# Summing the partial rows of the adaLN modulation: transposes and a VectorE reduction in place of float32 matmuls with a selector

## The chip, the cores and the metric

The kernel is written in a tile language for one Trainium2 chip and uses one of its cores. Times are device microseconds of one execution. TensorE (PE in the profile) does the matrix work, VectorE (DVE) and ScalarE (ACT) the elementwise work, GpSimd (POOL) some small steps, and SyncE (SP) issues most of the transfers.

## The reference

One layer of a diffusion backbone runs on 128 context tokens and 512 latent tokens, D_MODEL = 1024, all in float32. What matters here is the modulation (adaLN): two conditioning vectors, one for the latent tokens and one for the context, are turned into six vectors of 1024 each.

```python
mod = (jax.nn.silu(cond) @ w_ada + b_ada)[:, None, :]
sh1, sc1, g1, sh2, sc2, g2 = jnp.split(mod, 6, axis=-1)
h = _rms(x, norm_mix) * (1 + sc1) + sh1
mix, k, v = _mixer(h, rope, ctx_k, ctx_v, w_in, ...)   # attention and a gated convolution
x = x + g1 * mix
h2 = _rms(x, norm_ffn) * (1 + sc2) + sh2
gate, up = jnp.split(h2 @ w_gate_up, 2, axis=-1)
x = x + g2 * ((jax.nn.silu(gate) * up) @ w_down)
```

`sh1, sc1` are needed before the input projection of every token, `sh2, sc2` only before the feed-forward part.

## The kernel before

Activations lie with features on the partitions when they enter a matmul: `hH[k]` and `hL[k]` are the rounded high part and the remainder of the modulated input for the 128 features of block k (k = 0 to 7), 640 tokens wide. Most products are done as three matmuls on high and low parts (`mm3`, lines 155 to 157).

**The partial sums.** `cond_mm` (line 388) multiplies the two SiLU'd conditioning vectors, padded to 32 columns (`cp`), with a block of `w_ada`. The eight blocks of the contraction go to four different groups of 32 output rows (`g = k % 4`), so the result in PSUM has 128 rows: row 32 g + c holds a partial sum of group g for conditioning vector c, with c = 0, 1 in use. The four groups have still to be added, and the result has to be turned so that features lie on the partitions. Both are done by one float32 matmul for each 128 features: the copied rows `res` are the stationary operand and `sel[:, 0:2]` the moving one, where `sel` has a one in row 32 g + c of column c.

**Where this occurs.** First in the opening stage: the string P1SEQ lists its steps in order, and in it `a` k is `ada1_mm` (the partial sums of feature block k, shift and scale together), `b` k is `ada1_res` (VectorE copies them to `res`, line 433), `m` k is `ada1_mod` (two selector matmuls at line 440, then `mod_evict`), `h` k is `h_do` (ScalarE and VectorE make hF, hH and hL of block k from the turned input `xT`), and `q` k t is `q_mm` (the query projection of block k for the 128 tokens t). In this stage the order on VectorE, ScalarE, GpSimd and SyncE is that of the program too, as written in the string. Second in the attention and convolution stage: the generator `ada_all` (line 777) does the same for the sections 3 and 4 of the modulation, two halves of 512 columns each, four selector matmuls for one half, spread among the steps `F` of the string SEQ; the last half falls into the start of the output projection. There the order on TensorE is that of the program, and the order on the other engines is set by a scheduler with priorities.

**mod_evict** (lines 404 to 416) reads the sums: one VectorE multiplication with the norm gain into `modt` (line 411), an addition into `modA` (line 412), and an addition of the bias into `modB` (line 415). `h_do` uses modA and modB as scale and bias (lines 473 to 479).

**Other steps that the prediction names.** Line 323 loads the blocks `af` of w_ada for the opening stage, four buffers in turn, from SyncE's queue. Line 536 makes the low part `wl` of a loaded weight on VectorE, line 152 the low part of other split tiles (hL among them), line 248 that of the output projection's weights. Line 247 makes their high part on ScalarE. Line 834 is the exponential of attention (`pr`), 840 its division, 851 the transposes of `pr`, 868 the product with the values; line 875 evicts it to `t`, 890 adds its two halves to `of`, line 891 squares that to `osq`, which `att_rms` (line 940) sums with a column of ones on TensorE. Line 1220 is an addition of the feed-forward part.

Of the kernel before, what the change touches and what calls it, by code (L numbers as in the profile page):

```python
# [9 lines left out]
F32 = mybir.dt.float32  # L10
F32R = mybir.dt.float32r
AF = mybir.ActivationFunctionType
ALU = mybir.AluOpType
AX = mybir.AxisListType

P = 128
# [15 lines left out]
CG = 32  # L32
# [59 lines left out]
def build(ctx, tc, x_prompt, x_sample, c, cache_k, cache_v, c_ctx, norm_mix, norm_ffn, w_ada, b_ada,  # L92
# [3 lines left out]
    act, dve, pool, pe, sp = nc.scalar, nc.vector, nc.gpsimd, nc.tensor, nc.sync  # L96
# [23 lines left out]
    def T(tag, shape, dt=F32, bufs=1):  # L120
        seq[0] += 1
        return pools[where.get(tag, "A")][1].tile(list(shape), dt, tag=tag, bufs=bufs, name=f"{tag}_{seq[0]}")

    def PB(shape=(P, 512), dt=F32, tag="t"):
        seq[0] += 1
        if kept.get(tag):
            w = kept[tag].pop()
            n = 1
            for y in shape[1:]:
                n *= y  # L130
            w = w[:, :n] if tag != "s" else w
            if tag != "s" and len(shape) > 2:
                names = "abc"[:len(shape) - 1]
                w = w.rearrange("p (" + " ".join(names) + ") -> p " + " ".join(names), **dict(zip(names, shape[1:])))
            return w
        return pools["psum"][1].tile(list(shape), dt, tag=tag, bufs=pbufs[tag], name=f"p{tag}_{seq[0]}")
# [10 lines left out]
    def early(n):  # L147
        return tc.high_priority(n)
# [106 lines left out]
    def W(key):  # L255
        p = place[key]
        while not in_pre[0] and stream_at[0] < len(order):
            nxt = order[stream_at[0]][0][0]
            ahead = AO if nxt == "o" else AOP if nxt in ("g", "u", "op") else AHEAD
            if stream_at[0] > p + ahead or order[stream_at[0]][2] > phase[0]:  # L260
                break
            load_next()
        assert order[p][5] is not None, key
        return order[p][5]
# [33 lines left out]
    for gi, grp in enumerate(GROUPS):  # L298
# [5 lines left out]
        for j in range(2):  # L304
            for i0 in range(0, len(grp), 2):
                n = len(grp[i0:i0 + 2])
# [22 lines left out]
    ident = T("ident", (P, P))  # L329
# [52 lines left out]
    sel = T("sel", (P, CG))  # L382
# [3 lines left out]
    def cond_mm(out, k, w):  # L386
        g = k % 4
        pe.matmul(out[CG * g:CG * (g + 1)], cp[:, k], w, start=(k < 4), stop=(k >= KD - 4), skip_group_check=True)  # L388
# [16 lines left out]
    def mod_evict(i, f0, n, ps_sc, ps_sh):  # L405

        no = (V_MIX, V_FFN)[i]
        bo = (0, 24)[i]
        if ps_sc is not None:
            tmp = T("modt", (P, n, 2), F32, 2)  # L410
            dve.tensor_tensor(tmp, ps_sc, vec[:, no + f0:no + f0 + n].unsqueeze(2).to_broadcast([P, n, 2]), ALU.mult)
            dve.tensor_tensor(modA[i][:, f0:f0 + n, :], tmp,
                              nb[:, i, f0:f0 + n].unsqueeze(2).to_broadcast([P, n, 2]), ALU.add)
        if ps_sh is not None:
            dve.tensor_tensor(modB[i][:, f0:f0 + n, :], ps_sh,
                              vec[:, bo + f0:bo + f0 + n].unsqueeze(2).to_broadcast([P, n, 2]), ALU.add)
# [14 lines left out]
    def ada1_res(k):  # L431
        res = T("res", (P, 256), F32, 2)
        dve.tensor_copy(res, ada1[k])
        ada1[k] = res

    def ada1_mod(k):
        res = ada1.pop(k)
        mp = PB((P, 2, 1, 2), tag="c" if k < 2 else "t")
        for i in range(2):
            pe.matmul(mp[:, i, 0], res[:, i * P:(i + 1) * P], sel[:, 0:2], start=True, stop=True)  # L440
        mod_evict(0, k, 1, mp[:, 0], mp[:, 1])

    xT = T("xT", (P, KD, TOK))

# [132 lines left out]
    def q_evict(t):  # L577
# [3 lines left out]
        else:  # L581
            act.activation(qraw[t], qacc[t], AF.Copy)

    steps = {"r": x_norm, "s": x_scale, "c": late_consts, "w": w_hi, "l": w_lo, "p": lambda i: rows2_load(), "x": xT_do,
             "v": lambda i: (vec_do, vec2_do)[i](), "m": ada1_mod, "a": ada1_mm, "b": ada1_res, "d": spin,
             "n": h_rest, "E": q_evict, "R": lambda i: rope_tables()}
    in_pre[0] = True
    for x in P1SEQ.split():
        k = int(x[1:] if x[0] == "d" else x[1:2] or 0)
# [164 lines left out]
    def ada_all():  # L754
        for sec, j in ADA:
            rp = PB(tag="c")
            for h in range(4):
                w = W(("ada", sec, j, h))
                for i in range(2):
                    cond_mm(rp, 2 * h + i, w[:, i])  # L760
                if h == 1:
                    yield
            res = T("rs5", (P, 512))
            with early(RSP) if RSP else ExitStack():
                act.activation(res, rp, AF.Copy)
            if sec == 2:
                sp.dma_start(res[2:3], b_ada[0:1, sec * D + j * 512:sec * D + (j + 1) * 512])
            yield
            if sec == 2:
                for cc in range(2):  # L770
                    ps = PB(tag="c")
                    pe.matmul(ps, selT[:, cc], res, start=True, stop=True)
                    act.activation(g1[cc][:, j * 512:(j + 1) * 512], ps, AF.Copy)
            else:
                ps = PB((P, 4, 2), tag="c")
                for f in range(4):
                    pe.matmul(ps[:, f], res[:, f * P:(f + 1) * P], sel[:, 0:2], start=True, stop=True)
                if sec == 4:
                    mod_evict(1, 4 * j, 4, ps, None)
                else:  # L780
                    mod_evict(1, 4 * j, 4, None, ps)

    ada_gen = ada_all()

    def ada_some(n):
# [176 lines left out]
    for x in SEQ.split():  # L962
        if "." in x:
            n, i = (int(y) for y in x[1:].split("."))
# [347 lines left out]


tile_hymba = with_exitstack(build)

_INS = ["x_prompt", "x_sample", "c", "cache_k", "cache_v", "c_ctx", "norm_mix", "norm_ffn", "w_ada", "b_ada",
# [44 lines left out]
```

## Time and profile before

| | |
|---|---|
| Time, median of 3 runs | 758.66 us |
| Runs | 757.63, 758.73, 758.66 us |
| Profiled execution: from first to last instruction | 755.2 us |
| Profiled execution's own time outside the trace | not given; the median of the runs lies 3.46 us above the span |
| TensorE busy | 737.5 us, 98% |
| VectorE busy | 551.7 us, 73% |
| ScalarE busy | 378.8 us, 50% |
| Mean granted TensorE clock | 0.999 |

Busy times of TensorE overlap: a matmul's recorded duration includes time in which the next has begun, so the distance between the starts of neighbouring instructions tells what one costs. A float32 matmul appears as two records (two weight loads and two matmuls), a transpose and a matmul of the rounded type as one.

### The profile page before, as it was taken

Reading aid. Unit: us, or ns where it says so; the run is one execution under the profiler, and the core shown is the slowest. Engines: PE = TensorE matmul, PEld = TensorE weight load, DVE = VectorE, ACT = ScalarE, POOL = GpSimd, SP = SyncE. Lnnn points to the kernel's source line nnn. Section 1 sums busy time; section 2 is a strip of 40 time slices with the busy share of each in tenths; the row PEclk is TensorE's granted clock in tenths of the full one; section 3 lists DMA queues with packets and bytes.
Section 4 is the critical chain, followed back from the end, with each engine's and each line's share of the span. In section 5 each row is a group of like instructions: output and inputs, shape, how many; then the busy total and the mean of one; then the engine's idle time right before and its main releaser. Section 6 shows DMA issues by size and latency. Waiting matters only on the chain.

```text
span 755.2 us, 11953 instructions
## 1 busy us (share of the span) xinstructions
PE 737.5 (98%) x4618; PEld 665.2 (88%) x4618; DVE 551.7 (73%) x997; ACT 378.8 (50%) x745; POOL 42.6 (6%) x75
## 2 busy tenths in 40 slices
PE   7999899999999999999999999999999999999997
PEld 5678888988998887899998799998889998899986
DVE  5558877666666798779979778884678866788653
ACT  5356777667656534765552235553125541255410
POOL 2403101011000110100000000000000000000000
PEclk9999999999999999999999999999999999999999
DMA  9985133532432464031235313133113232222312
GB/s 290 294 236 163 51 104 102 165 92 91 159 107 91 133 224 138 1 112 54 81 118 157 108 58 110 58 111 112 56 56 104 67 112 78 62 86 84 112 56 83
DMA packets 101389, 84.52 MB, mean 112 GB/s; under 512 B 3502, under 2 KB 81650, under 8 KB 101332
## 3 DMA queue, kind: packets, MB, share of 16 engines
q1 hardware_dynamic: 100980, 83.39, 35.9%
q8 instruction: 36, 0.59, 0.3%
q0 software_dynamic: 352, 0.37, 0.3%
q14 instruction: 21, 0.17, 0.1%
HBM read 79.68 MB, written 2.75 MB: 109 GB/s over the span
## 4 chain that ended last, share of the span: by engine, by line
PE 83%; DVE 7%; ACT 5%; DMA 2%; issue 1%; SPq 1%; POOL 0%; ACTq 0%
PE pf L155 17%; PE pf L157 17%; PE pf L156 17%; PE pc L710 3%; PE pc L712 3%; PE pc L711 3%; PE po L868 3%; PE ps L824 2%; PE ph L155 2%; PE ph L157 2%; PE ph L156 2%; PE pc L388 2%; PE pt L851 2%; DMA wf<-in_w_in_dram 1%; PE ps L155 1%
## 5 line engine op out<-in xcount | busy, mean ns | idle before, releaser
L151 ACT ACTIVATE wh<-wf 128x512 fp32r<-128x512 f32 (+1 forms) x68 | 55.5, 816 | 81.1 <-PE pf L157 59.3
L155 PE MATMUL pf<-wh,gT 128*128 128x512 f32 (+1 forms) x225 | 86.9, 386 | 0.0
L156 PE MATMUL pf<-wl,gT 128*128 128x512 f32 (+1 forms) x225 | 86.5, 385 | 0.0
L157 PE MATMUL pf<-wh,gT 128*128 128x512 f32 (+1 forms) x225 | 86.5, 384 | 0.0
L710 PE MATMUL pc<-hH,wh 128*128 128x320 f32 x192 | 61.1, 318 | 0.0
L712 PE MATMUL pc<-hH,wl 128*128 128x320 f32 x192 | 59.3, 309 | 0.0
L711 PE MATMUL pc<-hL,wh 128*128 128x320 f32 x192 | 59.3, 309 | 0.0
L152 DVE TENSOR_TENSOR wl<-wf,wh 128x1024 fp32r<-128x1024 f32 (+1 forms) x34 | 39.4, 1160 | 25.2 <-ACT wh L151 22.1
L155 PE MATMUL pf<-T,wh 128*128 128x320 f32 x160 | 49.6, 310 | 0.5 <-ACT u L1191 0.5
L156 PEld LDWEIGHTS pf<-wl,gT 128*128 128x128 f32 x225 | 42.3, 188 | 8.6 <-issue 0.2
L155 PEld LDWEIGHTS pf<-wh,gT 128*128 128x128 f32 x225 | 42.3, 188 | 8.6 <-issue 0.2
L157 PEld LDWEIGHTS pf<-wh,gT 128*128 128x128 f32 x225 | 42.3, 188 | 8.3
L156 PE MATMUL pf<-T,wh 128*128 128x320 f32 x160 | 49.4, 309 | 0.0
L155 PE MATMUL pf<-T,wl 128*128 128x320 f32 x160 | 49.4, 309 | 0.0
L156 PE MATMUL pf<-T,wl 128*128 128x320 f32 x160 | 49.4, 309 | 0.0
L157 PE MATMUL pf<-T,wl 128*128 128x320 f32 x160 | 49.4, 309 | 0.0
L157 PE MATMUL pf<-T,wh 128*128 128x320 f32 x160 | 49.4, 309 | 0.0
L155 PE MATMUL pf<-B,wl 128*128 128x320 f32 x152 | 47.1, 310 | 0.0
L157 PE MATMUL pf<-B,wl 128*128 128x320 f32 x152 | 47.0, 309 | 0.0
L156 PE MATMUL pf<-B,wl 128*128 128x320 f32 x152 | 47.0, 309 | 0.0
L155 PE MATMUL pf<-B,wh 128*128 128x320 f32 x136 | 42.2, 310 | 1.5 <-DVE cu L1220 1.5
L151 ACT ACTIVATE wl<-wf 128x512 fp32r<-128x512 f32 x34 | 21.2, 625 | 41.6 <-PE pf L156 34.8
(306 smaller groups left out, 2058.7 us busy)
## 6 DMA issues: line engine op xcount, KB each, us to landing
wf<-in_w_gate_up_dram SPq DMA_DIRECT2D x44, 512.0 KB, 4.0
aw<-in_w_ada_dram SPq DMA_DIRECT2D x24, 512.0 KB, 4.1
wf<-in_w_down_dram SPq DMA_DIRECT2D x20, 512.0 KB, 3.3
wf<-in_w_in_dram SPq DMA_DIRECT2D x18, 512.0 KB, 5.5
af<-in_w_ada_dram SPq DMA_DIRECT2D x32, 256.0 KB, 6.4
x<-in_x_sample_dram SPq DMA_DIRECT2D x8, 512.0 KB, 6.2
wf<-in_w_out_dram SPq DMA_DIRECT2D x8, 512.0 KB, 4.4
wf<-in_w_ada_dram SPq DMA_DIRECT2D x8, 512.0 KB, 3.7
```

The source lines that it names most:

```text
L151: act.activation(hi, src, AF.Copy)
L152: dve.tensor_tensor(lo, src, f32(hi), ALU.subtract)
L155: pe.matmul(out, lh, rh, start=start, stop=False, skip_group_check=more)
L156: pe.matmul(out, lh, rl, start=False, stop=False, skip_group_check=more)
L157: pe.matmul(out, ll, rh, start=False, stop=stop, skip_group_check=more)
L388: pe.matmul(out[CG * g:CG * (g + 1)], cp[:, k], w, start=(k < 4), stop=(k >= KD - 4), skip_group_check=True)
L710: pe.matmul(acc, wh[:, k], hH[k][:, c0:c0 + n], start=(k == 0), stop=False)
L711: pe.matmul(acc, wh[:, k], hL[k][:, c0:c0 + n], start=False, stop=False)
L712: pe.matmul(acc, wl[:, k], hH[k][:, c0:c0 + n], start=False, stop=(k == KD - 1))
L824: pe.matmul(s2[:, g, :320], q, kk[:, v, P + g * 320:P + (g + 1) * 320], start=(i == 0), stop=(i == 1))
L851: pe.transpose(tp[:, i, h], u[3][h][:, kt * P:(kt + 1) * P], ident)
L868: pe.matmul(ov, w, x[:, i].rearrange("p a q -> p (a q)"), start=(g == 0 and i == 0 and n == 0), stop=(last and i == len(kts) - 1 and n == 1))
```

## The change

The function `mod_sum` turns each block of 128 columns of the partial rows by a TensorE transpose (the moving operand is the identity, the stationary one the rows, as before). The turned block in PSUM has for each feature (partition) 128 columns, of which column 32 g + c is the partial sum of group g for vector c. One VectorE reduction reads the eight columns with c = 0, 1 of each block and adds the four groups into `modt` in SBUF. `mod_evict` then reads `modt`, multiplies in place, and goes on as before. Tags and numbers of buffers are the same; the PSUM tile has 128 columns for each block in place of two. The selector `sel` stays, since the section for `g1` uses it.

```diff
@@ mod_evict
         if ps_sc is not None:
-            tmp = T("modt", (P, n, 2), F32, 2)
+            tmp = ps_sc
             dve.tensor_tensor(tmp, ps_sc, vec[:, no + f0:no + f0 + n].unsqueeze(2).to_broadcast([P, n, 2]), ALU.mult)
@@
+    def mod_sum(res, n, tag):
+
+        tp = PB((P, n, P), tag=tag)
+        for i in range(n):
+            pe.transpose(tp[:, i], res[:, i * P:(i + 1) * P], ident)
+        out = T("modt", (P, n, 2), F32, 2)
+        dve.tensor_reduce(out, tp.rearrange("p i (g c) -> p i c g", c=CG)[:, :, 0:2], AX.X, ALU.add)
+        return out
+
     def ada1_mod(k):
         res = ada1.pop(k)
-        mp = PB((P, 2, 1, 2), tag="c" if k < 2 else "t")
-        for i in range(2):
-            pe.matmul(mp[:, i, 0], res[:, i * P:(i + 1) * P], sel[:, 0:2], start=True, stop=True)
-        mod_evict(0, k, 1, mp[:, 0], mp[:, 1])
+        mp = mod_sum(res, 2, "c" if k < 2 else "t")
+        mod_evict(0, k, 1, mp[:, 0:1], mp[:, 1:2])
@@ ada_all
             else:
-                ps = PB((P, 4, 2), tag="c")
-                for f in range(4):
-                    pe.matmul(ps[:, f], res[:, f * P:(f + 1) * P], sel[:, 0:2], start=True, stop=True)
+                ps = mod_sum(res, 4, "c")
                 if sec == 4:
```

The order of the built program changes with it. TensorE keeps its order, with a transpose at the place of each of the 32 selector matmuls. VectorE gets 12 reductions. In the attention stage the scheduler moves some neighbours: on ScalarE the eviction of line 875 and the squaring of line 891 (once each, of the same tile `of`) come later than before among their neighbours, and VectorE takes one pair of instructions ahead of an addition of line 890; some accumulations of the second gate change places with each other.

## Prediction

> **What bounds the kernel now.** I read the page first (busy shares, chain), then the windows by stage, then the timeline of each engine around the changed lines.
>
> ```profile
> PE 737.5 (98%) x4618; PEld 665.2 (88%) x4618; DVE 551.7 (73%) x997; ACT 378.8 (50%) x745; POOL 42.6 (6%) x75
> ...
> PE 83%; DVE 7%; ACT 5%; DMA 2%; issue 1%; SPq 1%; POOL 0%; ACTq 0%
> ```
>
> TensorE holds 83% of the chain that ends last. So TensorE time saved is time saved, except where another engine or a transfer sets the pace. The windows tell where (columns: length; busy PE, weight load, DVE, ACT, POOL; clock, DMA share, GB/s):
>
> ```profile
> 24.00:34.20 10.20, 9.71 (x67) 6.25 (x64) 5.41 (x14) 4.68 (x7) 3.65 (x10) 1.00 1.12 292
> 34.20:60.00 25.80, 25.80 (x158) 18.96 (x159) 15.08 (x35) 13.51 (x19) 0.00 (x0) 1.00 0.91 262
> 60.00:112.00 52.00, 47.32 (x352) 43.05 (x350) 41.88 (x110) 38.33 (x98) 9.42 (x12) 1.00 0.32 92
> ...
> 186.00:217.00 31.00, 31.00 (x235) 28.02 (x234) 19.79 (x40) 20.48 (x44) 1.12 (x2) 1.00 0.32 107
> ```
>
> Until 34 us the DMA engines are full (share 1.12). From 34.2 to 60 and from 186 to 217 TensorE has no gap at all. From 60 to 112 it idles 4.7 us behind VectorE and ScalarE.
>
> **What the change removes on TensorE.** There are eight steps `m` with two selector matmuls and four half sections with four: 32 matmuls. The 16 of the half sections make this row, two records for each, so it is 64 records in all:
>
> ```profile
> L777 PE MATMUL pc<-sel,rs x32: 165/251/251, 186.1 to 264.0; 128*128 128x2 f32 x32
> ```
>
> The 251 ns overlap; the price comes from the starts of the neighbours.
>
> ```profile
> 24.62 0.39 PE L157 MATMUL pc<-wh,hL 128*128 128x512 f32 x1
> 24.85 0.50 PE L440 MATMUL pt<-sel,res 128*128 128x2 f32 x4
> 25.21 0.47 PE L155 MATMUL ps<-wh,hH 128*128 128x512 f32 x1
> 25.53 0.39 PE L156 MATMUL ps<-wl,hH 128*128 128x512 f32 x1
> ```
>
> ```profile
> 214.84 0.31 PE L712 MATMUL pc<-hH,wl 128*128 128x320 f32 x1
> 214.99 0.95 PE L777 MATMUL pc<-sel,rs 128*128 128x2 f32 x8
> 215.87 1.07 PE L388 MATMUL pc<-aw,cp 128*32 128x512 f32 x8
> ```
>
> From L157 to L156 are 0.91 us; the two ordinary steps in it take 0.23 each (24.62 to 24.85), so the four records cost 0.45. Eight cost 215.87 - 214.84 - 0.15 = 0.88. A record costs 0.11 us. Transposes of the new form (128x128 float32, identity moving) stand in the same kind of stream:
>
> ```profile
> 218.96 0.31 PE L712 MATMUL pc<-hH,wl 128*128 128x320 f32 x1
> 219.11 1.04 PE L851 MATMUL pt<-ident,pr 128*128 128x128 f32 x8
> 219.91 0.39 PE L710 MATMUL pc<-hH,wh 128*128 128x320 f32 x1
> 220.13 0.31 PE L711 MATMUL pc<-hL,wh 128*128 128x320 f32 x1
> ```
>
> These eight records are eight transposes: 220.13 - 218.96 less two steps of 0.15 leaves 0.87, again 0.11 each. So 32 transposes give 32 records in place of 64: 0.22 us less for each step `m`, 0.44 less for each half section, 8 x 0.22 + 4 x 0.44 = 3.5 us of TensorE time.
>
> **What it adds on VectorE.** Twelve reductions over 16 or 32 PSUM elements, with the next instruction waiting for the result. No such row exists. The nearest:
>
> ```profile
> 3.72 0.36 DVE L383 TENSOR_REDUCE sel<-ident 128x32 f32<-128x128 f32 x1
> ...
> 15.84 0.15 DVE L411 TENSOR_TENSOR modt<-pc,vec 128x2 f32<-128x2 f32 x1
> 16.03 0.16 DVE L412 TENSOR_TENSOR modA<-modt,nb 128x2 f32<-128x2 f32 x1
> ```
>
> It lies between a two-element operation (0.15; the dependent one starts 0.19 after it) and the reduction of 128 elements (0.36). I take 0.2, being much nearer to the small one; with hand-over 0.15 to 0.4 remain for the range. It cannot be below nothing, as it is an added instruction. The Trainium skill speaks against such a step: "VectorE: DVE Perf Modes", section "Rules for kernel authors", calls a reduction on the hot path the slowest operation of VectorE, at one element a cycle. The row of L383 agrees that it isn't cheap; at 16 elements the rate weighs little, and by the page's errata table (120 cycles plus one for each element, at 0.96 GHz) I get an estimate of 0.14 us, which would move the sum by under 0.1.
>
> **Step by step, what reaches the end.**
>
> m0 (15 us): L411 follows other VectorE work, not TensorE, so the reduction delays modB and ScalarE's hH by up to 0.2. m1 to m3 save 0.66. Neither lasts, because the next blocks of w_ada arrive when the full DMA engines bring them:
>
> ```profile
> 30.77 0.64 PE L388 MATMUL pc<-af,cp 128*32 128x256 f32 x8 [0.32 <-DMA af<-in_w_ada_dram]
> ```
>
> ```profile
> 34.17 0.64 PE L388 MATMUL pc<-af,cp 128*32 128x256 f32 x8 [0.17 <-DMA af<-in_w_ada_dram]
> ```
>
> I count 0 (0.66 gained if the loads come earlier too, because SyncE's issues wait for TensorE to free `af`).
>
> m4 to m7: 4 x 0.22 = 0.88 in a stretch with no gap. Only the last is tight; hL of block 7 is needed by its third matmul:
>
> ```profile
> 55.49 0.82 DVE L152 TENSOR_TENSOR hL<-hF,hH 128x640 fp32r<-128x640 f32 x1 [1.28 <-ACT hH L151]
> ```
>
> ```profile
> 56.95 0.39 PE L157 MATMUL ps<-wh,hL 128*128 128x512 f32 x1
> ```
>
> hL ends at 56.31, 0.64 early. TensorE comes 0.44 earlier against it (m6, m7), the reduction takes 0.2: just used up, 0.05 may be lost. Gain 0.85. The stretch from 60 to 112 starts from TensorE's key projection and has none of the new instructions, so I carry the gain through.
>
> Half sections at 186, 215 and 244: 0.44 each, 1.32. Their modA and modB are used only in the next stage, and VectorE idles often here, so the reductions hide. The fourth (263) saves 0.44 as well, but there VectorE is only just in time with the last low part of the output weights:
>
> ```profile
> 292.08 0.74 DVE L248 SCALAR_TENSOR_TENSOR wl<-wf,vec,wh 128x512 fp32r<-128x512 f32 x1
> ```
>
> ```profile
> 293.08 0.40 PE L156 MATMUL ph<-wl,mx 128*128 128x512 f32 x1
> ```
>
> It ends at 292.82, 0.26 before its use, so I count 0.25 of the 0.44.
>
> The reordered ScalarE. Before, one high part of a weight (L247) follows the eviction L875, for which ScalarE idles 0.77:
>
> ```profile
> 217.99 0.38 ACT L875 ACTIVATE t<-po 128x256 f32<-128x256 f32 x1 [0.77 <-PE po L868]
> 218.27 0.71 ACT L247 ACTIVATE wh<-wf,vec 128x512 fp32r<-128x512 f32 x1
> ...
> 224.01 0.42 ACT L891 ACTIVATE osq<-of 128x256 f32<-128x256 f32 x1 [0.66 <-DVE of L890]
> ...
> 225.72 0.87 ACT L834 ACTIVATE pr<-ps,nsr,rq 128x640 f32<-128x640 f32 x1
> ```
>
> ```profile
> 222.09 0.39 PE L868 MATMUL po<-pl,VS 128*128 128x256 f32 x1 [0.50 <-DVE pl L152]
> ```
>
> ```profile
> 226.02 0.95 PE L940 MATMUL pt<-ones,osq 128*128 128x1 f32 x8
> ```
>
> Moved into that idle time, L247 lets the exponential and the low part behind it come some 0.6 earlier, and the 0.50 of TensorE at 222.09 goes. But L891 now comes after L834, which started at 225.72 and takes 0.87. With L834 about 0.4 earlier, as VectorE's maximum for it passes L890, osq is finished near 225.7 - 0.4 + 0.9 + 0.4 = 226.6, while att_rms, then at 225.5, wants it about 0.4 after its start: a wait of about 0.6 replaces that of 0.50. I count 0, with -0.4 to +0.5 for the range. What is queued behind that wait is the value product and the next scores, which feed the chain of attention.
>
> **Sum.** 0.85 + 1.32 + 0.25 + 0 = 2.4 us. The page gives the profiled execution only as its span, 755.2; the runs' median of 758.66 lies 3.46 above it. The sum is made in the span (755.2 to 752.8), and the same difference is taken off the median: 756.3 us. A measurement of this kernel tells about 0.2% (1.5 us) from no change.
>
> **Rivals.**
>
> *Swallowed.* Less reaches the end, because VectorE and ScalarE set the pace from 60 to 112 and VectorE again further on, where TensorE waits for it:
>
> ```profile
> 363.19 0.41 PE L155 MATMUL pf<-B,wh 128*128 128x320 f32 x1 [1.48 <-DVE cu L1220]
> ```
>
> If the gain before 60 us is lost to VectorE's and ScalarE's own queues, 1.3 + 0.25 are left, and with the worst of osq (0.4) 1.2: 757.5. Against it: both queues there start from TensorE's projection. Chance 0.17.
>
> *More.* The loads of w_ada come earlier (0.66) and the wait at 222.09 goes without a new one (0.5): 2.4 + 1.2 = 3.6, 755.1. Against it: share 1.12 of the DMA engines in that window. Chance 0.10.
>
> *It doesn't do what it says.* A transpose of float32 is issued in two records like the matmul, so nothing is saved on TensorE, and m0's and m7's reductions cost 0.2 + 0.05: 758.9. The eight records of L851 for eight transposes speak against it. In the Trainium skill, "FP8 and Floating Point Precision", section "Matmul Precision", gives true float32 four passes through the array; by that rule moving 128 columns rather than 2 would eat the gain. The trace shows 0.11 us for a transposed record, so the rule doesn't carry over to transposes here. Chance 0.04.
>
> *Slower.* The reduction costs the 0.36 of L383 plus 0.05 of hand-over, and in each of the eight steps `m` it lands on the path: VectorE's queue hands hL(k) later than TensorE wants it. Then TensorE's gain of the opening stage is lost in waits and 8 x 0.41 = 3.3 us are added, less 1.57 of the half sections: 760.4. It decides where the slack of hL(k) is under 0.41; block 7 has 0.64 now, or 0.2 after the shift, and for the earlier blocks the string has a whole step `a` and several `q` more between `h` and their first `q`. So one block may show it, not eight. Chance 0.06.
>
> **How the numbers follow.** Forecast 0.63 (own range 755.6 to 757.1, by the terms' bounds); rivals 0.17, 0.10, 0.04, 0.06. The range of 8 in 10 takes the forecast, the swallowed case and most of the larger gain, with half a microsecond for the spread of the runs (757.63 to 758.73): 754.9 to 758.2. Faster by over 0.2% means under 757.14: nearly all of the forecast (0.59), the larger gain (0.10) and a little of the swallowed case (0.03): 0.72. Slower by over 0.2% (above 760.18): 0.05 of the slower case and 0.01 of others, 0.06. The rest, 0.22, is the same.
>
> **What would show it.** Line 440 in the new profile should have 32 records, one for each transpose, with the neighbours' starts 0.69 (not 0.91) apart around a pair and 0.59 (not 1.03) around four; TensorE's busy time lower by 3 to 4 us. Line 442 should take 0.15 to 0.26 in twelve instances. The gap at 222.09 should be gone and one before L940 (new line 945) be there. The gaps at 30.77 and 34.17 should grow by what m1 to m3 save. The prediction is wrong if L442 is over 0.36, if line 440 has 64 records, if hL waits show before several `q`, or if the wait of line 1220 at 363 grows by what TensorE gained.

## The result and the profile after

The changed kernel takes 755.63 us (median of 6 runs, 755.17 to 756.43); the kernel before took 758.51 us beside it (6 runs, 757.63 to 759.36). The ratio is 0.9964, 95% interval 0.9954 to 0.9974: 2.9 us less, against a forecast of 2.4. The profiled execution took 755.84 us with a span of 754.0 us, so 1.8 us lie outside the span. By that measure the first profile of the kernel before (span 755.2) was an execution of some 757.0 us, less than any of its 83 timed runs in this study (lowest 757.07). The pair of profiles therefore shows only 1.2 of the 2.9 us. This matters for everything below.

Busy times and the chain, from the page of the changed kernel:

```profile
PE 735.5 (98%) x4586; PEld 661.6 (88%) x4586; DVE 553.2 (73%) x1009; ACT 378.7 (50%) x745; POOL 42.7 (6%) x75
...
PE 82%; DVE 8%; ACT 5%; DMA 3%; issue 1%; SPq 0%; POOL 0%; ACTq 0%; DVEq 0%
```

TensorE has 32 records fewer, and DMA has 3% of the chain in place of 2%. The windows answer to those of before:

```profile
24.00:34.20 10.20, 9.28 (x60) 5.63 (x63) 5.73 (x16) 5.39 (x8) 3.74 (x10) 1.00 1.14 296
34.20:60.00 25.80, 25.75 (x156) 18.25 (x149) 16.28 (x40) 13.69 (x20) 0.00 (x0) 1.00 0.91 266
60.00:112.00 52.00, 46.83 (x346) 42.32 (x345) 41.31 (x110) 37.75 (x96) 9.43 (x12) 1.00 0.31 88
186.00:217.00 31.00, 31.00 (x232) 27.77 (x232) 19.02 (x41) 20.61 (x44) 1.52 (x2) 1.00 0.33 107
```

From 60 to 112 us TensorE is busy 46.83 us, 0.49 less than before in a window of the same length: it idles more there. The new instructions, from the views of lines 440 and 442 (duration in ns, least, median, most):

```profile
L440 PE MATMUL pc<-ident,rs x16: 270/272/273, 186.1 to 262.7; 128*128 128x128 f32 x16
...
L440 PE MATMUL pt<-ident,res x12: 270/272/327, 24.7 to 52.1; 128*128 128x128 f32 x12
...
L440 PE MATMUL pc<-ident,res x4: 272/273/273, 15.0 to 22.0; 128*128 128x128 f32 x4
```

```profile
L442 DVE TENSOR_REDUCE modt<-pc x6: 165/178/192, 15.7 to 266.7; 128x8 f32<-128x32 f32 x4, 128x4 f32<-128x16 f32 x2
L442 DVE TENSOR_REDUCE modt<-pt x6: 165/175/175, 26.3 to 53.0; 128x4 f32<-128x16 f32 x6
```

16 + 12 + 4 are 32 records for 32 transposes, and twelve reductions of 0.16 to 0.19 us. Around a pair and around four, TensorE's timeline of the changed kernel reads:

```profile
24.43 0.39 PE L157 MATMUL pc<-wh,hL 128*128 128x512 f32 x1
24.67 0.38 PE L440 MATMUL pt<-ident,res 128*128 128x128 f32 x2
24.80 0.48 PE L155 MATMUL ps<-wh,hH 128*128 128x512 f32 x1
25.12 0.40 PE L156 MATMUL ps<-wl,hH 128*128 128x512 f32 x1
...
214.44 0.31 PE L719 MATMUL pc<-hH,wl 128*128 128x320 f32 x1
214.59 0.60 PE L440 MATMUL pc<-ident,rs 128*128 128x128 f32 x4
215.12 1.07 PE L388 MATMUL pc<-aw,cp 128*32 128x512 f32 x8
```

L157 to L156 takes 0.69 (before 0.91). L719 to L388 takes 0.68 (before 1.03), not 0.59: a half section saves 0.35, not 0.44.

**Where the time went.** Setting each matmul of the changed kernel beside the same one of the kernel before gives TensorE's lead (negative: the changed kernel is earlier). The first column of leads is against the first profile, the second against a later profile of the kernel before, whose span of 756.7 us is a usual one (control2 below):

```
near us   what lies just before            lead, span 755.2   lead, span 756.7
  34.5    m0 to m3, loads of w_ada              -0.20              -0.38
  57      m4 to m7                              -0.71              -0.88
  92      the K/V turn                          +0.03              -0.13
 187.5    half section at 186                   -0.30              -0.47
 217.5    half section at 215                   -0.74              -0.88
 222.5    value product (wait for pl)           -1.14              -1.28
 227      att_rms (wait for osq)                -0.59              -0.75
 228.5    next scores (wait for pr)             -0.60              -1.80
 230      transposes of pr, right behind        -0.60              -2.11
 245.5    half section at 244                   -0.94              -2.46
 265      half section at 263                   -1.40              -2.92
 end                                            -1.14              -2.64
```

The opening's 0.7 to 0.9 us is lost at 91 us. Here is the addition on VectorE before, which started without a wait, and then, of the changed kernel, the addition that waits and TensorE's wait behind it:

```profile
88.85 0.42 DVE L889 TENSOR_TENSOR of<-t,es 64x256 f32<-64x256 f32 x1
```

```profile
88.90 0.42 DVE L894 TENSOR_TENSOR of<-t,es 64x256 f32<-64x256 f32 x1 [0.70 <-DMA es<-t]
...
89.81 0.42 DVE L664 CAST KB<-pt 128x256 fp32r<-128x256 f32 x1
```

```profile
91.06 0.41 PE L829 MATMUL ps<-KB,qT 128*128 128x320 f32 x1 [0.44 <-DVE KB L664]
```

The `es` transfer carries half of a tile from one half of the partitions to the other. It goes in two pieces. They were issued 0.68 us earlier than before (by 86.54 in place of 87.22), and the second landed at 89.11 in place of 89.02. The trace has sixteen landing signals for each piece. For the second, fifteen of them came by 88.21 us, 0.80 earlier than before (89.01), and the last one 0.90 later; before, it came 0.01 later. In the changed kernel a single packet of 8 KB, of the kind `instruction`, starts at 87.08 us in the middle of the transfer; before, it started at 88.28, when the transfer was nearly over. The last section says what these packets are. Further on, the wait at 222.09 shrank, the wait of att_rms came, and the wait of line 1220 (now 1225) stayed:

```profile
220.95 0.39 PE L873 MATMUL po<-pl,VS 128*128 128x256 f32 x1
...
225.77 0.61 PE L945 MATMUL pt<-ones,osq 128*128 128x1 f32 x4 [0.37 <-ACT osq L896]
...
362.05 0.42 PE L155 MATMUL pf<-B,wh 128*128 128x320 f32 x1 [1.47 <-DVE cu L1225]
```

The steps of 1.05 us at the scores and of 0.31 at the transposes behind them are in the second column alone, and no part of the change is there. The experiments went after them.

### The profile page after: what moved, and what is told of

It reads as the page before. It is cut to its first block, busy times and chain, and to the rows that moved or that the text cites. A ratio compares the mean times of both kernels' runs of the same rounds, so it can differ in the third digit from the quotient of the medians.

```text
span 754.0 us, 11900 instructions
## 1 busy us (share of the span) xinstructions
PE 735.5 (98%) x4586; PEld 661.6 (88%) x4586; DVE 553.2 (73%) x1009; ACT 378.7 (50%) x745; POOL 42.7 (6%) x75
## 4 chain that ended last, share of the span: by engine, by line
PE 82%; DVE 8%; ACT 5%; DMA 3%; issue 1%; SPq 0%; POOL 0%; ACTq 0%; DVEq 0%
PE pf L155 17%; PE pf L156 17%; PE pf L157 17%; PE pc L717 3%; PE pc L719 3%; PE pc L718 3%; PE ph L155 2%; PE ph L156 2%; PE ph L157 2%; PE po L873 2%; PE ps L829 2%; PE pt L856 2%; PE pc L388 2%; DMA es<-t 1%; ACT pr L839 1%
## 5 line engine op out<-in xcount | busy, mean ns | idle before, releaser
L156 PE MATMUL pf<-wl,gT 128*128 128x512 f32 (+1 forms) x225 | 86.5, 385 | 0.0
L157 PE MATMUL pf<-wh,gT 128*128 128x512 f32 (+1 forms) x225 | 86.5, 384 | 0.0
L719 PE MATMUL pc<-hH,wl 128*128 128x320 f32 x192 | 59.3, 309 | 0.0
L157 PEld LDWEIGHTS pf<-wh,gT 128*128 128x128 f32 x225 | 42.3, 188 | 8.5
L156 PEld LDWEIGHTS pf<-wl,gT 128*128 128x128 f32 x225 | 42.3, 188 | 8.4 <-issue 0.2
L156 PE MATMUL pf<-T,wl 128*128 128x320 f32 x160 | 49.4, 309 | 0.0
L157 PE MATMUL pf<-T,wl 128*128 128x320 f32 x160 | 49.4, 309 | 0.0
L156 PE MATMUL pf<-T,wh 128*128 128x320 f32 x160 | 49.4, 309 | 0.0
L157 PE MATMUL pf<-T,wh 128*128 128x320 f32 x160 | 49.4, 309 | 0.0
L157 PE MATMUL pf<-B,wl 128*128 128x320 f32 x152 | 47.0, 309 | 0.0
L156 PE MATMUL pf<-B,wl 128*128 128x320 f32 x152 | 47.0, 309 | 0.0
L1275 DVE TENSOR_TENSOR dm<-pf,g 128x512 f32<-128x512 f32 (+1 forms) x41 | 27.7, 676 | 21.1 <-PE pf L157 21.1
```

The costliest lines, as they stand in the source:

```text
L156: pe.matmul(out, lh, rl, start=False, stop=False, skip_group_check=more)
L157: pe.matmul(out, ll, rh, start=False, stop=stop, skip_group_check=more)
L719: pe.matmul(acc, wl[:, k], hH[k][:, c0:c0 + n], start=False, stop=(k == KD - 1))
L1275: dve.tensor_tensor(dm, ps[:, :n], g2[cc][:, oc], ALU.mult)
```

## The experiments

Four theories. **A**: TensorE's records are the price, and the opening's saving reaches the end. **B**: that saving is swallowed by the `es` transfer at 89 us. **C**: the reductions lie on the path. **F** (formed after the first four runs): the change moved the loads of TensorE's own code away from an `es` transfer. All runs in one table. The last three columns are of the profiled execution: the start of the one code load (a 16 KB packet) between 214 and 226 us, the first and last 512-byte packet of the `es` transfer issued near 219 us (both from the trace's packet records), and the start of the addition that waits for it.

```
kernel        median us (runs)  ratio to before (95%)      span   code load  es packets      addition
before        758.51 (6)        1                          755.2  217.0      221.05-222.66   223.10
control       758.15 (11)       0.9998 (0.9988 to 1.0008)  755.4  217.0      221.05-222.88   223.35
control3      757.27 (1)                                   755.5  217.3      221.38-222.98   223.40
control2      758.47 (1)                                   756.7  217.6      221.97-224.08   224.62
after_fetch   757.89 (11)       0.9996 (0.9982 to 1.0010)  754.9  219.6      220.66-222.92   223.41
half_only     757.66 (11)       0.9994 (0.9985 to 1.0003)  755.9  220.1      220.89-223.30   223.76
open_only     758.51 (11)       0.9999 (0.9990 to 1.0008)  756.2  221.7      221.36-223.52   224.11
half_fetch2   756.24 (11)       0.9979 (0.9970 to 0.9987)  754.0  222.2      220.04-221.29   221.82
after         755.63 (6)        0.9964 (0.9954 to 0.9974)  754.0  223.1      220.33-221.75   222.40
twice_dve     755.33 (5)        0.9961 (0.9948 to 0.9973)  753.4  223.1      220.12-221.49   222.06
half_fetch    756.45 (11)       0.9979 (0.9970 to 0.9987)  755.3  223.3      220.77-222.23   222.93
twice_half    757.18 (11)       0.9987 (0.9979 to 0.9996)  755.3  223.7      221.32-222.64   223.19
r2_later      755.52 (7)        0.9968 (0.9957 to 0.9979)  754.2  223.8      220.93-222.33   222.93
twice_open2   756.19 (11)       0.9976 (0.9967 to 0.9984)  755.2  224.1      221.69-222.88   223.43
```

**The kernel before again (control).** No edit.

> The kernel before, unchanged. Every theory expects a difference of 0 +- 0.3 us; its profile is a second look at the kernel before. The first profiled run had a span of 755.2 us, which with the 1.8 us outside the span of the changed kernel's runs would be 757.0 us, under all six timed runs (757.63 to 759.36). Theory A (TensorE's records are the price, and the opening stage's saving reaches the end): the second profile has a longer span, 756 to 757 us, and loses the rest between 60 and 112 us or in the first 34 us. Theory B (the opening's saving is swallowed by the es transfer, which landed at 89.0 us in one profile and 89.1 in the other though it was issued 0.68 us earlier): span 755.2 again and the es transfer lands at 89.0 again.

Ratio 0.9998, 758.15 us. The second profile again came from the low end of the runs (757.12, lowest of 11; highest 760.26). It could not say where the usual runs lose more.

**The opening alone (open_only).** With it the first product of `mod_evict` gets a tile of its own again where the selector is used, here and in half_only.

```
             else:
-                ps = mod_sum(res, 4, "c")
+                ps = PB((P, 4, 2), tag="c")
+                for f in range(4):
+                    pe.matmul(ps[:, f], res[:, f * P:(f + 1) * P], sel[:, 0:2], start=True, stop=True)
```

> Transposes and reductions only in the eight blocks of the opening stage; the half sections keep the selector matmuls, and the order on ScalarE is that of the kernel before. Theory A: 16 records of 0.11 us are gone, of which those of m4 to m7 count: -0.85 us against the kernel before (-1.5 if m1 to m3 count too). Theory B: 0 to -0.2 us, with a wait of the es transfer before the KB addition near 88.9 us that eats the gain. Theory C (the reductions are on the path): +0.2 us or more.

No change at all: 0.9999. The same wait at 89 us is there:

```profile
89.22 0.42 DVE L896 TENSOR_TENSOR of<-t,es 64x256 f32<-64x256 f32 x1 [0.59 <-DMA es<-t]
```

A's -0.85 did not come. B accounts for that by itself: the 8 KB packet, at 87.42 us here, lies in the transfer as it does in the changed kernel, and one landing signal of sixteen is 0.68 us late. F adds that the 16 KB code load (221.7) sits in the middle of the later `es` transfer.

**The half sections alone (half_only).** The edit is the reverse one, in `ada1_mod`.

```
-        mp = mod_sum(res, 2, "c" if k < 2 else "t")
-        mod_evict(0, k, 1, mp[:, 0:1], mp[:, 1:2])
+        mp = PB((P, 2, 1, 2), tag="c" if k < 2 else "t")
+        for i in range(2):
+            pe.matmul(mp[:, i, 0], res[:, i * P:(i + 1) * P], sel[:, 0:2], start=True, stop=True)
+        mod_evict(0, k, 1, mp[:, 0], mp[:, 1])
```

> Transposes and reductions only in the four half sections; the opening stage keeps the selector matmuls; ScalarE's order is that of the changed kernel. Theory A: 16 records of 0.11 us gone, -1.6 to -1.8 us against the kernel before, with the wait of 0.50 us at 222 us down to 0.1 and one of 0.4 us before att_rms (line 945 of the changed kernel, +2 or so here). Theory B: nearly the whole gain of the changed kernel, -2.2 to -2.9 us. Theory C: the same as A.

0.7 us by the medians (0.9994, and the interval takes in no change), where A and B wanted 1.6 to 2.9. The two halves of the change give 0 and 0.7, and together 2.9: they do not add up, which no theory of TensorE's records allows. Its profile shows the wait of att_rms at 1.27 us, not 0.37, and behind it a late `es`:

```profile
223.76 0.42 DVE L896 TENSOR_TENSOR of<-t,es 64x256 f32<-64x256 f32 x1 [1.82 <-DMA es<-t]
...
227.11 0.61 PE L947 MATMUL pt<-ones,osq 128*128 128x1 f32 x4 [1.27 <-ACT osq L898]
```

The low part, the maximum and the second addition queue behind this addition on VectorE; the exponential (L841) and `osq` on ScalarE wait for them. In the packet records of this run a single 16 KB packet of another kind starts at 220.1 us and takes 0.89 us, just ahead of `es`. The page of the changed kernel counts these packets in its list of DMA queues (packets, MB, share of 16 engines):

```profile
q8 instruction: 36, 0.59, 0.3%
```

36 packets of 16 KB for 4,586 matmuls and as many weight loads: some 255 TensorE records for each. They come every 15 to 31 us, with 215 to 298 TensorE records (median 250) started between two of them and 19 to 54 VectorE instructions, so it is TensorE's work that sets their distance. Fewer TensorE records ahead of a place move them later. From this came theory F.

The late `es` is not the whole difference, though. In the traces half_only ends 1.84 us behind the changed kernel: 0.9 arise from 222 to 228 us, 0.4 from 188 to 217 us, where VectorE waits 0.35 us for an earlier `es` transfer, and 0.6 at 352 us (more on that place under half_fetch2).

**Each reduction twice (twice_dve).**

```
         dve.tensor_reduce(out, tp.rearrange("p i (g c) -> p i c g", c=CG)[:, :, 0:2], AX.X, ALU.add)
+        dve.tensor_reduce(out, tp.rearrange("p i (g c) -> p i c g", c=CG)[:, :, 0:2], AX.X, ALU.add)
```

> The changed kernel with every one of its twelve reductions issued twice (the second writes the same result again). Theory A and B: a reduction takes 0.17 to 0.19 us beside TensorE's work, so the time stays that of the changed kernel within 0.3 us (-2.6 to -2.9 us against the kernel before). Theory C: each reduction lies on the path, so 12 x 0.18 = 2.1 us come back (about -0.8 us against the kernel before).

755.33 us, ratio 0.9961. Twelve more reductions cost nothing that the times can tell. The traces show more. In block 7 the low part hL comes too late for TensorE already in the changed kernel, and the second reduction makes it later (the changed kernel, then twice_dve):

```profile
55.25 0.83 DVE L152 TENSOR_TENSOR hL<-hF,hH 128x640 fp32r<-128x640 f32 x1 [1.27 <-ACT hH L151]
56.13 0.50 PE L157 MATMUL ps<-wh,hL 128*128 128x512 f32 x1
```

```profile
55.76 0.83 DVE L152 TENSOR_TENSOR hL<-hF,hH 128x640 fp32r<-128x640 f32 x1 [1.27 <-ACT hH L151]
56.64 0.50 PE L157 MATMUL ps<-wh,hL 128*128 128x512 f32 x1
```

TensorE loses 0.45 us of its lead there, in place of 0.2, and at 57 us it is 0.5 us behind the changed kernel. That comes back at 91 us: with the added VectorE instructions the 8 KB packet starts at 83.49 us, ahead of the `es` transfer, whose sixteen signals now arrive without a late one, and at 92 us TensorE is 0.1 us ahead of the changed kernel. So C is out for the sum of the twelve, and with it the prediction's rival on the slower side; one block shows it, as that rival had allowed. The Trainium skill's rule against such a step ("VectorE: DVE Perf Modes", section "Rules for kernel authors", a reduction as the slowest operation) does not bite at 16 and 32 elements: 0.16 to 0.19 us, against the 0.14 that the prediction worked out from the same page.

**The code loads moved back by warm-up products alone (after_fetch).** `dN` in the order P1SEQ issues N products of the identity with itself, which nothing reads.

```
-... r3 v0 d4 x2 ... x3 m0 d4 w ...
+... r3 v0 d7 x2 ... x3 m0 d8 w ...
```

> The changed kernel with seven more of the warm-up products that TensorE issues in its idle time before 17 us (28 more TensorE instructions, 1.5 us of work ahead of loads that end later anyway). Nothing else moves. Theory F: TensorE's code is loaded in 36 packets of 16 KB, each about 1 us on a DMA engine; the removed records moved the one that fell at 217.0 us in the kernel before (at 221.7 and 220.1 us with half of the change) to 223.1 us, behind the es transfer of 220.3 to 221.8 us that VectorE waits for. Here it should come back to about 220.9 us, the es transfer should end about 1 us later, and the time should be 0.8 to 1.5 us above the changed kernel (-1.4 to -2.1 us against the kernel before). Theory A (records alone are the price): the time of the changed kernel, -2.9 us.

757.89 us: 2.3 us of the 2.9 are gone, by work put into the start, which made TensorE 0.43 us later at 34.5 us and 0.13 later at 92. The code load went to 219.6, the addition to 223.41, and att_rms waits again:

```profile
223.41 0.42 DVE L894 TENSOR_TENSOR of<-t,es 64x256 f32<-64x256 f32 x1 [1.57 <-DMA es<-t]
...
226.77 0.61 PE L945 MATMUL pt<-ones,osq 128*128 128x1 f32 x4 [1.03 <-ACT osq L896]
```

F's direction is met and its size exceeded (0.8 to 1.5 expected); this kernel's profile, second fastest of its 11 runs, shows 0.9 us of it. Of the sixteen landing signals of the first piece of `es`, for which the addition waits, fifteen came by 222.31 us and the last at 223.39, so one part in sixteen was 1.08 us late.

**The code loads moved away from half_only (half_fetch, half_fetch2).** Nine warm-up products fewer; in half_fetch2 twelve of them become three of 512 columns, which keep TensorE as busy with fewer instructions.

```
-'d11 r0 ... v0 d4 ... m0 d4 ...
+'d8 r0 ... v0 d1 ... m0 d1 ...                      (half_fetch)
+'d203 r0 ... v0 d100 ... m0 d4 ...                  (half_fetch2; each hundred is one wide product)
+            pe.matmul(qacc[-1].rearrange("p (a q) -> p a q", q=P), ident,
+                      ident.unsqueeze(1).to_broadcast([P, 4, P]), start=True, stop=True)
```

> The kernel with transposes in the half sections alone, with nine warm-up products fewer before 17 us (36 TensorE instructions fewer). Theory F: the code load that fell at 220.1 us moves to about 223 us, as in the changed kernel; the es transfer takes 1.1 to 1.5 us again instead of 2.4, the wait of att_rms for osq falls from 1.27 to about 0.4 us, and the time comes within 0.5 us of the changed kernel (-2.2 to -2.9 us against the kernel before, where half_only had -0.6). Theory A: the time of half_only, -0.6 us, as no record that counts is removed; perhaps worse for the colder start.

> half_only with 36 TensorE instructions fewer before 17 us, as in half_fetch, but TensorE kept as warm: twelve warm-up products of 128 columns become three of 512 columns. half_fetch had the granted clock at 0.90 from 17 to 34 us and was 0.6 us late at 91 us against the changed kernel for it. Theory F: clock 1.00 there, the code load of 220.1 us again at about 223 us, osq wait 0.4 us, and the time within 0.3 us of the changed kernel if the opening's saving is swallowed at 89 to 91 us (-2.6 to -2.9 us against the kernel before), or 0.6 to 0.9 us above it if it is not (-2.0 to -2.3). Theory A: as half_only, -0.6 us.

756.45 and 756.24 us, where half_only has 757.66: warm-up products alone bring 1.2 to 1.4 us by the medians (1.1 by the ratios). The `es` transfer lands early, and att_rms runs through without a wait (half_fetch2):

```profile
221.82 0.42 DVE L899 TENSOR_TENSOR of<-t,es 64x256 f32<-64x256 f32 x1 [0.58 <-DMA es<-t]
...
224.64 1.15 PE L950 MATMUL pt<-ones,osq 128*128 128x1 f32 x8
```

Against the kernel before beside them they are at -2.0 and -1.8, short of what F had asked (-2.2 to -2.9 for the first; for the second -2.6 to -2.9, or -2.0 to -2.3 if the opening's saving reaches the end). half_fetch had the colder start: the windows of both from 17 to 34 us have the granted clock at 0.90 and at 1.00.

```profile
17.00:34.00 17.00, 16.19 (x103) 10.21 (x104) 10.77 (x26) 6.04 (x10) 9.74 (x18) 0.90 1.15 295
```

```profile
17.00:34.00 17.00, 15.87 (x112) 9.78 (x112) 10.83 (x27) 7.03 (x12) 8.82 (x18) 1.00 1.16 294
```

half_fetch2 is also the test of the opening: it has the selector there, and the changed kernel has not. At 92 us it is no later than the changed kernel (0.2 us earlier), which is B. By the medians it is 0.6 us slower; the two profiled spans are both 754.0. The traces show a further place where the two kernels differ. At 293 us half_fetch2 is 0.69 us ahead of the changed kernel, and at 363 us they are level. ScalarE waits longer for a block of the next weight (half_fetch2, then the changed kernel), ScalarE and VectorE hand pieces to each other from there on, and at 352 us TensorE waits for them (half_fetch2):

```profile
325.75 0.63 ACT L151 ACTIVATE wh<-wf 128x512 fp32r<-128x512 f32 x1 [1.39 <-DMA wf<-in_w_gate_up_dram]
```

```profile
325.74 0.63 ACT L151 ACTIVATE wh<-wf 128x512 fp32r<-128x512 f32 x1 [0.67 <-DMA wf<-in_w_gate_up_dram]
```

```profile
352.49 0.42 PE L155 MATMUL pf<-T,wh 128*128 128x320 f32 x1 [0.75 <-ACT p L1201]
```

An 8 KB packet starts at 323.99 us, inside the load of half_fetch2, and one of that load's sixteen landing signals is 0.80 us late. half_only and half_fetch have the same (packets at 325.83 and 325.21, 0.80 and 0.84 late); no other run has the packet in the load or a signal over 0.37 late. These three kernels have eight VectorE instructions fewer than the changed one, so the comparison by their times doesn't isolate the opening.

**The opening's price put back (twice_open2).** Each transpose of the opening twice, eight warm-up products fewer.

```
             pe.transpose(tp[:, i], res[:, i * P:(i + 1) * P], ident)
+            if n == 2:
+                pe.transpose(tp[:, i], res[:, i * P:(i + 1) * P], ident)
```

> The changed kernel with each transpose of the opening stage issued twice (16 more, the TensorE price of the selector matmuls is back there), and eight warm-up products fewer before 17 us, so that the count of TensorE's instructions after the opening is that of the changed kernel and its code loads fall where they fell (223.1 us). Theory B (the opening's saving is swallowed by the es transfer of 89 us): the time of the changed kernel within 0.3 us, -2.6 to -2.9 us against the kernel before. Theory A: 0.85 us of it is lost, -2.0 us.

756.19 us, 0.6 above the changed kernel, between B and A. It does not tell them apart: this start was cold as well (clock 0.90), TensorE came 1.05 us late into 34.5 us, and m4 to m7 took 0.8 more.

**The half sections' price put back (twice_half).** As above with `n == 4`, four warm-up products fewer. A second line differs, in the output projection: a step that prepares part of a feed-forward operand (`b_plain`) runs at `n == 4` in place of `n == 2`, which changes the order of a few instructions on ScalarE and VectorE from 308 to 316 us.

> The changed kernel with each transpose of the half sections issued twice (16 more; their TensorE price is back), and four warm-up products fewer before 17 us, so that the code load of about 223 us stays within 1.3 us of its place (222.5 to 224 us, time base included). Theories A and F: 4 x 0.44 = 1.76 us are lost, -1.1 us against the kernel before; the remaining gain is the code load's. A theory in which TensorE's records in the half sections count for nothing: -2.9 us.

757.18 us, 1.55 above the changed kernel. TensorE falls back by 0.44 in each of the four sections (1.76). Some 0.3 of it is made up at 222 us, where it no longer waits for `pl`, and 0.4 from 293 to 363 us; its trace ends 1.23 us behind the changed kernel's. The second line can have a part in the 0.4, but not in the four steps of 0.44. A and F hold for the half sections.

**Two more looks at the kernel before (control2, control3).** No edit.

> The kernel before once more, one look: where do its usual runs lose the 1.1 us by which their median span (756.5 us) lies above the two profiled spans (755.2, 755.4)? Theory F: in es transfers that land later than in those two profiles (89.0, 202.0, 223.1 to 223.4 us), above all the one at 219.7 us, whose landing decides when the maximum behind it on VectorE can start. Theory A: in TensorE's own time or in the loads of the first 34 us.

> As control2: a second look at the kernel before. Theory F: a span over 756 us goes with an es transfer of 219.7 us that lands after 223.5 us; a span near 755.3 us with one that lands before.

758.47 and 757.27 us, a usual and a quick execution. From 34.5 to 225.5 us TensorE runs within 0.15 us of control in control2; then the `es` transfer lands late, the maximum (L830) behind it starts late, and the scores wait for the exponential. VectorE, then TensorE, of control2:

```profile
224.62 0.42 DVE L889 TENSOR_TENSOR of<-t,es 64x256 f32<-64x256 f32 x1 [1.85 <-DMA es<-t]
225.07 0.42 DVE L890 TENSOR_TENSOR of<-t,es 64x256 f32<-64x256 f32 x1
225.52 0.42 DVE L152 TENSOR_TENSOR pl<-pt,ph 128x256 fp32r<-128x256 f32 x1
225.87 0.81 DVE L830 TENSOR_REDUCE nsr<-ps 128x1 f32<-128x640 f32 x1
```

```profile
228.25 0.56 PE L824 MATMUL ps<-KA,qT 128*128 128x320 f32 x2 [0.79 <-ACT pr L834]
```

At this one place control2 loses 1.1 of the 1.3 us by which its span exceeds control's, and F had named it. The bound of 223.5 us held for both looks, taken for the landing that the addition waits for (223.38 and 224.60 us). Why `es` is late here is not shown. It is not one late signal as in after_fetch: the first piece's signals run from 222.66 to 224.60 us and the fifteenth comes 0.01 before the last. The 16 KB code load is a little later than in control (217.6 for 217.0), and the issue of the `aw` block ahead of `es` takes 1.32 us in place of 0.88 (0.42 in the changed kernel, which has no code load there).

**att_rms later (r2_later).** The one version that the waits suggested.

```
-... O12.1 F1 F1 r2 O12.2 S14.0 ...
+... O12.1 F1 F1 O12.2 r2 S14.0 ...
```

> The changed kernel with att_rms of tile 2 put behind the value product that follows it on TensorE (two products, some 0.25 us), and nothing else moved. Its wait for osq (0.37 us at 225.8 us) should fall to about 0.1 us, and the time by 0.25 us at most, -3.1 us against the kernel before; where the es transfer lands late, the value product no longer waits behind att_rms. If the wait for osq is hidden anyway by VectorE's and ScalarE's chain, the time stays that of the changed kernel.

The wait is gone (the eight products run from 225.75 us on without a gap), but the time is that of the changed kernel (755.52 to 755.63 us; 0.9968, 0.9957 to 0.9979). The 0.25 us can't be told from the spread.

## Why the forecast held, and which of its reasons did

- **Record price and counts: right.** 32 records in place of 64, 0.11 us each by the neighbours' starts (0.69 around a pair, as foretold). The foretold 0.59 around four was 0.68, as the product after them (L388) starts 0.09 late. TensorE's busy time fell by 2.0, not by 3 to 4; the sections account for 3.1 (8 x 0.2 and 1.5). I don't know where the rest of the busy time is.
- **m0 to m3, counted 0: right at the end.** The DMA waits at 30.8 and 34.2, 0.49 together, became one of 0.79. They took 0.3 of the 0.66 saved; 0.2 to 0.4 us reached 34.5 us, and nothing of it passed 92 us.
- **m4 to m7, -0.85: too large at 57 us, and nothing of it at 92.** From 34.5 to 57 us the lead grew by 0.5. Four pairs saved 0.8, 0.1 went at 39 us and 0.2 in the wait for hL of block 7, for which the sum had 0.05. TensorE then leads by 0.7 to 0.9, with what m0 to m3 left, and by 0 to 0.1 at 92 us. The step that failed is "so I carry the gain through": the stretch has none of the new instructions, but it has a transfer whose landing did not move, because its last landing signal came late, as in every kernel that had an 8 KB code packet in the middle of this transfer and in no other. This is the outcome of the swallowed case, through `es` and not through VectorE's and ScalarE's own queues. Whether some of the opening survives in the usual runs stays open: the 0.6 us between half_fetch2 and the changed kernel (756.24 against 755.63) contain half_fetch2's own loss at 325 us.
- **Half sections, 1.32 + 0.25: right in sum.** 0.35 each for three, and the fourth 0.46, of which 0.11 is lost at 292 us: 1.4. Putting their price back costs 1.55 by the medians. Not in the sum: a further 0.15 of TensorE's lead is lost at 352 us, where ScalarE and VectorE set the pace.
- **The reordered ScalarE, counted 0: right.** The wait of 0.50 became 0.11, and one of 0.37 came before line 945 (I had put 0.6); together +0.15. But I took the landing of `es` as given. Its bounds of -0.4 to +0.5 were too narrow: with a late `es` the wait of att_rms is 1.03 (after_fetch) to 1.27 (half_only).
- **Not in the sum: the landing of `es` near 222 us.** Of the lead of 2.64 against a usual execution (control2, one profile), 1.36 come at 228.5 to 230 us, where the kernel before waits behind a late `es` and the changed one doesn't. So 2.9 us is, as far as the runs tell, about 1.5 of the half sections, 1 to 1.4 of this landing, and 0 to 0.6 of the opening (0 to 0.1 by the traces). That the landing follows the code loads is shown for the loads of 219.6 to 221.7 us; for the kernel before, with its load at 217.0 to 217.6, it is argued. The forecast of 2.4 was near by luck: the opening's 0.85 that didn't arrive was replaced by 1 us or more that it didn't know of.
- **A sign that I had passed over.** I put the 3.46 us between the median and the span down as lying around the span. 1.8 lie outside it; 1.6 said that the execution I read was quicker than the usual one, and so that something in it varies.

## What to carry to other kernels

Time saved on the busiest engine counts only up to the next transfer that lands when it landed before; follow the saving to the first wait for a DMA, even through a stretch that the change does not touch. Before a sum is made, compare the profiled execution with the timed runs: if it is quicker than all of them, the usual cost has to be found elsewhere. When an edit changes how many instructions an engine has, try the same edit with idle instructions added or taken away, on each engine whose count changes, before its gain is put down to the work removed.

## What the runs showed that I had not expected

- TensorE's code comes in packets of 16 KB, 0.9 to 1.1 us each near 220 us, while data transfers run. When one started at 219.6 to 221.7 us, the `es` transfer took 2.2 to 2.4 us from its first packet to its last, and one of the sixteen landing signals of its first piece came 1.0 to 1.1 us after the other fifteen. With the load at 222.2 us or later it took 1.2 to 1.5, and no signal was more than 0.23 late. At 217.0 to 217.6 it took 1.6 to 2.1; there one signal was 0.74 late in control, and all were late in control2, the slowest. The records don't name the engine of a packet, so that the code load and the late part share one fits these numbers but is argued.
- Packets of 8 KB, of the same kind, go with the instructions of other engines:

```profile
q14 instruction: 21, 0.17, 0.1%
```

  Nine of the 21, the one at 87.08 us among them, come 121 to 133 VectorE instructions apart in the changed kernel, so the twelve reductions move them. They explain two places that the table of code loads does not. At 87 us one lies inside the `es` transfer in the six kernels that have the opening's eight reductions once (after, open_only, after_fetch, r2_later, twice_open2, twice_half), and one signal of the first piece is 0.37 to 0.83 us late. In the other eight it starts before the transfer or near its end, and no signal is more than 0.17 late. At 324 to 326 us the same happens to the three kernels with reductions in the half sections alone.
- Warm-up products that nothing reads were worth +2.3 us in one place (after_fetch) and -1.4 us in another (half_fetch2 against half_only).
- With four to nine warm-up products fewer before 17 us the granted clock from 17 to 34 us was 0.90 in place of 1.00, and TensorE came 0.7 to 1.1 us later into 34.5 us than in the changed kernel. Three products of 512 columns kept it at 1.00.
